# Head of a hybrid attention/pooling block: pooling weights fold first, mixer weights' two parts kept in DRAM for the second chunk

## The chip, the cores and the metric

One core of a Trainium2 chip runs one program. The metric is the device time of one execution in microseconds (us). Engines: PE (TensorE, matmul; PEld is its weight load), DVE (VectorE), ACT (ScalarE), POOL (GpSimd), SP (SyncE, which here issues every DMA). PSUM holds matmul results, SBUF everything else on the core, DRAM the rest.

## The reference, cut to what matters

```python
h = rmsnorm(x, attn_norm);  z = h @ w_in        # x: 2048 x 1024, fp32
u_pool, q, k, v, gates = split(z)               # 1024 | 16x64 | 2x64 | 2x64 | 2048
a = pool_mixer(u_pool)    # 4 groups of 256 channels: mean over the last 2/4/8/16 rows
                          # minus the row, then a 256x256 map per group (w_pool), scale
q, k = rope(rmsnorm(q)) / 8, rope(rmsnorm(k))   # rotary on 16 of 64 dims, by position
b = window attention(q, k, v)                   # window 128, 16 heads on 2 kv heads, sinks
x = x + (sigmoid(g_pool) * a + sigmoid(g_attn) * b) @ w_out
x = x + (silu(gate) * value) @ w_down           # up = causal conv3(rmsnorm(x) @ w_up)
```

## The kernel before

The 2048 rows are worked in two chunks of 1024. A chunk runs through a mixer (all of attention and pooling), the output projection, the up projection and the down projection. Activations lie transposed (channels on partitions), so a projection has a weight slab as its stationary operand and 512 columns of `h` as its moving one.

Every fp32 product is made of three passes. `split` writes a matrix as a high part (a cast on ACT to fp32r) and a low part (the difference, on DVE), and `mm3` multiplies high by high, high by low and low by high. A weight of 512 KB so becomes a tile of 1 MB in the pool "U" (19 buffers), which all big tiles share; raw weights arrive in the pool "R" (3 buffers). Other pools are "M" (5), "F" (4) and "Q" (4). Both chunks load and split the same mixer weights.

`Stream` serves the weights in the order of `weight_order()`: `get` of entry i issues the loads up to entry i+2 (`fetch`) and splits entries i+1 and i+2 (`part`), the latter often a little later. The pooling map is folded into the pooling part of `w_in` before its use: `fold(j)` multiplies half a group's input weights (`w_poolT[j]`) by the group's map (`w_pool`), 4 x 6 matmuls of 256 columns into two PSUM buffers "f", copies the sums to SBUF, and every second fold stores two slabs to `wfold` in DRAM, from which they are loaded later as slab kind "pu".

The mixer of a chunk first makes keys and values in 8 blocks of 128 rows (`raw`: 24 matmuls of 256 columns; `block`: norm, rotary, split; `turn`: transposes), with `first_fillers` between the blocks to keep PE busy: five of the eight folds and two slabs of the attention gate ("ga"). Then four groups of four heads follow, 8 items each, with gate slabs, pooling slabs and the other three folds between (`fillers`). A pooling slab of group g needs log2(window) doublings over 1024 columns on DVE, so one for group 0 and four for group 3; `windows` queues them in `slow`, two to a `run_later`.

In the program's head x arrives three times over: as `xT` in pieces for `h` (`make_h`, ACT for the high part and DVE for the low), and as rows for the sums of squares (`squares`, ACT), from which POOL makes the norm `r1` (`norm1`). `rope_tables` computes sine and cosine for all 16 blocks on DVE, with two Sin on ACT.

The order of instructions on each engine comes from a scheduling layer: program order is a priority, and it places an instruction where its tiles are expected to be free. Each engine then runs its own list strictly in order and waits on semaphores. That holds for SP too: a DMA that must wait for a buffer holds up those behind it.

Of the kernel before, what the change touches and what calls it, by code (L numbers as in the profile page):

```python
# [26 lines left out]
P = 128  # L27
# [17 lines left out]
FOLD_FIRST = 5  # L45


PRE = {0: 0, 1: 4}

# [23 lines left out]
class Stream:  # L73


    def __init__(self, entries, load, split):
        self.entries, self.load, self.split = entries, load, split
        self.raws, self.tiles = {}, {}
        self.used = self.loaded = self.parted = 0
# [29 lines left out]
def fillers(c, q4):  # L109

    ga = [[("ga", ct, n) for n in range(2)] for ct in (2 * q4 + 2, 2 * q4 + 3) if q4 < 3]
    pg = [[("pg", ct, n) for n in range(2)] for ct in (2 * q4 - 2, 2 * q4 - 1) if q4 > 0]
    pu = [[("pu", ct, n) for n in range(2)] for ct in (2 * q4, 2 * q4 + 1)]
    fold = [[("fold", j, 0)] for j in range(FOLD_FIRST, 8) if c == 0 and q4 == 0]
# [4 lines left out]
def first_fillers(c):  # L119

    ga = [("ga", ct, n) for ct in range(2) for n in range(2)]
    if c > 0:
        return [ga[0:1], [], ga[1:2], [], ga[2:3], [], ga[3:4], []]
    fold = [("fold", j, 0) for j in range(FOLD_FIRST)]
    return [fold[0:1], ga[0:1], fold[1:3], fold[3:4], fold[4:5], ga[1:2], ga[2:3], ga[3:4]]


def weight_order():
    out = []
    for c in range(NCH):  # L130
        if c > 0:
            out.append(("kv",))
        out += [(kind, j) for parts in first_fillers(c) for kind, j, n in parts if n == 0]
        out.append(("q", 0))
        for q4 in range(4):
            for n, parts in enumerate(fillers(c, q4)):
                if n == NB - 3 and q4 < 3:
                    out.append(("q", q4 + 1))
                out += [(kind, j) for kind, j, h in parts if h == 0]
        out += [("pg", ct) for ct in (6, 7)]  # L140
# [27 lines left out]
def block_kernel(ctx: ExitStack, tc: tile.TileContext, x, xT, pos, vec, qkn, w_poolT, w_pool, w_q, w_kv,  # L168
# [46 lines left out]

    def load_weights(kind, *a):
        if kind == "kv":
            srcs = [w_kv[:, 4 * j:4 * j + 4, :] for j in range(2)]
        elif kind == "q":
# [15 lines left out]
    def split_weights(key, raws):  # L235
# [4 lines left out]
        out = []  # L240
        for raw in raws:
            shape = [P, 2] + list(raw.shape)[1:]
            if key[0] in ("kv", "q"):
                out.append(up_.tile(shape, F32R, "U"))
            else:
                p, tag = (mp, "M") if out else (up_, "U")
# [79 lines left out]
    stream = Stream(weight_order(), load_weights, split_weights)  # L326
# [8 lines left out]
    posi = fp.tile([P, 16], I32, "F")  # L335
    load(posi, pos)
    vc = cp.tile([P, V_N], F32, "vc")
    load(vc, vec)

# [18 lines left out]

    def load_kv(i):
        raws.append(rp.tile([P, 4, 2 * P], F32, "R"))  # L360
# [9 lines left out]

    hs, kvw, raws = [], [], []
    for j in range(4):
        load_x0(j, 0, 256)
    for i in range(2):
        load_kv(i)
    gains = fp.tile([P, 2, HD], F32, "F")
    load(gains, qkn.rearrange("p (a d) -> p a d", a=2))
    make_h(0, 0, hs)
    for i in range(2):
        split_kv(i)  # L380
    stream.fetch(2)
# [4 lines left out]
    one = cp.tile([P, 1], F32, "one")  # L386
    V.memset(one, 1.0)
# [32 lines left out]
    tabs = {}  # L420

    def rope_tables():
        n = [P, 16, 8]
        posf = fp.tile([P, 16], F32, "F")
        V.tensor_copy(posf, posi)
        fr = fp.tile([P, 8], F32, "F")
        for i, f in enumerate(FREQ):
            V.memset(fr[:, i:i + 1], f)
        rt = up_.tile([P, 10, 16, 8], F32, "U")
# [7 lines left out]

        def reduced(dst, src, c):

            V.tensor_scalar(dst, src, c, None, op0=ALU.mult)  # L440
            rnd(s, dst)
            V.tensor_sub(dst, dst, s)
# [14 lines left out]
        for src, c in ((n0, a0), (n1, a1), (n2, a2), (n2, b2)):  # L457
            reduced(u, src, c)
            V.tensor_add(t, t, u)
        for i, off in ((8, 0.0), (9, 0.25)):  # L460
            V.tensor_scalar(u, t, off, None, op0=ALU.add)
            rnd(s, u)
            V.tensor_sub(u, u, s)
            V.tensor_scalar(u, u, 0.5 - 2.0**-25, -(0.5 - 2.0**-25), op0=ALU.min, op1=ALU.max)
            A.activation(rt[:, i], u, AF.Sin, scale=tau)
        sin, cos = rt[:, 8], rt[:, 9]

        gk = cp.tile([P, HD], F32, "gk")
        V.tensor_scalar(gk, gains[:, 1], 8.0, None, op0=ALU.mult)
        V.tensor_mul(gk[:, 16:HD], gk[:, 16:HD], gains[:, 0, 16:HD])  # L470
        tabs["gk"] = gk
        c = cp.tile([P, 16, 16], F32, "cq")
        sn = cp.tile([P, 16, 16], F32, "sq")
        for h in range(2):
            own = gains[:, 0, 8 * h:8 * h + 8].unsqueeze(1).to_broadcast(n)
            other = gains[:, 0, 8 - 8 * h:16 - 8 * h].unsqueeze(1).to_broadcast(n)
            V.tensor_tensor(c[:, :, 8 * h:8 * h + 8], cos, own, op=ALU.mult)
            V.tensor_tensor(sn[:, :, 8 * h:8 * h + 8], sin, other, op=ALU.mult)
        V.tensor_scalar(sn[:, :, 0:8], sn[:, :, 0:8], -1.0, None, op0=ALU.mult)
        tabs["q"] = (c, sn)  # L480
        ck = cp.tile([P, 16, 2, 8], F32, "ck")
# [921 lines left out]
```

## Time and profile before

| | |
|---|---|
| time, 3 runs | 2476.62, 2480.01 (median), 2482.35 us |
| profiled execution: its own time, its span | 2486.34 us, 2484.5 us |
| PE busy | 2433.9 us (98%) |
| DVE, ACT busy | 1967.4 us (79%), 1181.0 us (48%) |
| granted PE clock, mean | 0.996 |
| moved by DMA | 249.78 MB, mean 101 GB/s |

The span runs from the first to the last instruction; the profiled execution's own time is 1.8 us longer. Matmuls are pipelined: one of 512 columns reads as about 390 ns long, while they follow each other at about 227 ns, so group times are read as the busy time of the group and not as count times mean. The chunks' stages lie at: mixer 0 to about 540 us, output and up projection to about 1050, down projection to about 1270, then the same again.

### The profile page before, as it was taken

The page shows a single profiled execution, that of the slowest core. Times are in us where ns is not written, and L with a number is a line of the kernel's source. Part 1 is how long each engine was busy: PE and PEld are TensorE (multiplying, and loading weights), DVE is VectorE, ACT ScalarE, POOL GpSimd, SP SyncE. Part 2 cuts the span into 40 slices and gives each one's busy share as a digit, 9 for nine tenths or more (in the row PEclk, how much of TensorE's full clock was granted, in tenths as well). Part 3 has the DMA queues.
Part 4 walks back from the last instruction along what each step waited for, and adds up shares of the span by engine and source line. Part 5 has one row for each costly group of instructions (what it writes and reads, how often), then busy time and mean ns, then how long its engine had stood idle before and what let it go on. Part 6 is the DMA issues. An engine that isn't in the chain of part 4 may idle for free.

```text
span 2484.5 us, 32982 instructions
## 1 busy us (share of the span) xinstructions
PE 2433.9 (98%) x12224; PEld 2056.0 (83%) x12224; DVE 1967.4 (79%) x3528; ACT 1181.0 (48%) x2342; POOL 222.5 (9%) x217
## 2 busy tenths in 40 slices
PE   6999999999999999999999999999999999999999
PEld 6888888877888888788889888887788888887887
DVE  8776777885888788799966777778569788788994
ACT  6444444444455555543524444445435555454432
POOL 0122222200000000000002222222000000000000
PEclk9999999999999999999999999999999999999999
DMA  6221111038422233445231011110552222218321
GB/s 245 98 86 35 35 43 43 26 127 270 171 82 89 85 111 111 174 165 195 85 111 35 26 36 51 35 35 23 165 194 94 85 77 94 85 68 279 124 80 51
DMA packets 89871, 249.78 MB, mean 101 GB/s; under 512 B 9584, under 2 KB 11888, under 8 KB 87408
## 3 DMA queue, kind: packets, MB, share of 16 engines
q1 hardware_dynamic: 89712, 247.69, 28.9%
q8 instruction: 96, 1.57, 0.3%
q14 instruction: 63, 0.52, 0.1%
HBM read 196.28 MB, written 51.38 MB: 100 GB/s over the span
## 4 chain that ended last, share of the span: by engine, by line
PE 79%; DVE 13%; ACT 3%; DMA 2%; issue 2%; SPq 0%; POOL 0%; DVEq 0%; ACTq 0%; POOLq 0%
PE f L210 20%; PE f L954 18%; PE t L954 9%; PE a L210 6%; PE a L954 4%; PE f L1244 4%; PE a L1244 4%; PE t L1244 4%; PE s L1244 4%; ACT Q L711 1%; PE a L744 1%; PE s L690 1%; DVE F L794 1%; DVE U L195 1%; DVE U L840 1%
## 5 line engine op out<-in xcount | busy, mean ns | idle before, releaser
L210 PE MATMUL f<-U,U 128*128 128x512 f32 x3072 | 725.6, 393 | 8.9 <-ACT U L194 5.0
L210 PEld LDWEIGHTS f<-U,U 128*128 128x128 f32 x3072 | 573.6, 189 | 131.4 <-ACT U L194 8.6
L954 PE MATMUL f<-U,U 128*128 128x512 f32 x1512 | 359.7, 390 | 1.5 <-ACT Q L972 1.3
L954 PEld LDWEIGHTS f<-U,U 128*128 128x128 f32 x1512 | 283.4, 188 | 61.7 <-ACT Q L972 2.2
L1020 DVE SCALAR_TENSOR_TENSOR M<-F,vc,M 128x1024 f32<-128x1024 f32 x176 | 224.8, 1281 | 129.5 <-ACT M L1017 129.2
L210 PE MATMUL a<-U,U 128*128 128x256 f32 x1920 | 249.7, 285 | 12.9 <-ACT U L194 11.3
L210 PEld LDWEIGHTS a<-U,U 128*128 128x128 f32 x1920 | 242.4, 192 | 20.9 <-ACT U L194 11.3
L954 PE MATMUL t<-U,U 128*128 128x512 f32 x1080 | 254.2, 389 | 0.0
L954 PEld LDWEIGHTS t<-U,U 128*128 128x128 f32 x1080 | 202.7, 188 | 42.1
L711 ACT ACTIVATE Q<-s,st,r 128x128 f32<-128x128 f32 x256 | 114.4, 453 | 175.1 <-DVE st L706 167.4
L603 POOL TENSOR_TENSOR r<-r,mhalf 128x4 f32<-128x4 f32 (+1 forms) x80 | 77.2, 966 | 950.0 <-DVE r L602 888.3
L195 DVE TENSOR_TENSOR U<-R,U 128x512 fp32r<-128x512 f32 x214 | 146.3, 711 | 13.7 <-ACT U L194 12.8
L294 ACT CAST U<-R 128x1024 fp32r<-128x1024 f32 x120 | 125.4, 1053 | 65.9 <-DVE R L315 33.9
L295 DVE TENSOR_TENSOR U<-R,U 128x1024 fp32r<-128x1024 f32 x120 | 146.6, 1222 | 0.5 <-ACT U L294 0.5
L194 ACT CAST U<-R 128x512 fp32r<-128x512 f32 x214 | 123.2, 619 | 41.1 <-PE f L210 27.8
L954 PE MATMUL a<-U,U 128*128 128x512 f32 x576 | 138.6, 389 | 0.0
L954 PE MATMUL f<-U,M 128*128 128x512 f32 x504 | 123.9, 394 | 4.0 <-DVE F L998 4.0
L954 PEld LDWEIGHTS a<-U,U 128*128 128x128 f32 x576 | 108.0, 188 | 22.3
L1203 ACT CAST U<-U 128x1024 fp32r<-128x1024 f32 x74 | 77.2, 1051 | 86.2 <-PE a L1244 26.4
L954 PEld LDWEIGHTS f<-U,M 128*128 128x128 f32 x504 | 95.5, 190 | 24.8 <-DVE F L998 4.9
L1006 ACT COPY F<-f 128x512 f32<-128x512 f32 x42 | 24.7, 588 | 181.0 <-PE f L954 181.0
L1017 ACT ACTIVATE M<-F,vc 128x1024 f32<-128x1024 f32 x88 | 109.3, 1243 | 1.3
(253 smaller groups left out, 3902.5 us busy)
## 6 DMA issues: line engine op xcount, KB each, us to landing
R<-w_up SPq DMA_DIRECT2D x80, 512.0 KB, 3.3
actd<-M SPq DMA_DIRECT2D x44, 512.0 KB, 2.6
U<-w_down SPq DMA_DIRECT2D x88, 256.0 KB, 5.1
U<-actd SPq DMA_DIRECT2D x88, 256.0 KB, 5.4
R<-w_out SPq DMA_DIRECT2D x32, 512.0 KB, 4.3
U<-kept SPq DMA_DIRECT2D x12, 1024.0 KB, 7.8
R<-w_ga SPq DMA_DIRECT2D x16, 512.0 KB, 3.3
R<-w_q SPq DMA_DIRECT2D x16, 512.0 KB, 3.3
```

The lines of the kernel that those rows point to most:

```text
L194: A.copy(hi[:, t], src[:, t])
L195: V.tensor_sub(lo[:, t], src[:, t], hi[:, t].bitcast(F32))
L210: nc.tensor.matmul(out, a, b, start=(i == 0), stop=(i == n - 1))
L294: A.copy(t[:, 0], raw)
L295: V.tensor_sub(t[:, 1], raw, t[:, 0].bitcast(F32))
L603: G.tensor_tensor(r, r, mhalf[:, 0:nh], op=ALU.pow)
L711: A.activation(pr[:, h, :], sc[:, h, 0:P], AF.Exp, bias=nm[:, h:h + 1], scale=it["rq"][:, h:h + 1], accum_out=rs[:, h:h + 1])
L954: nc.tensor.matmul(bank, a[:, x, k, :], b[k // 2][:, y, k % 2, :], start=(first and i == 0), stop=(i == 11), skip_group_check=True)
L1017: A.activation(y, u[:, 2:], AF.Identity, bias=cw[:, 3, m:m + 1], scale=cw[:, 2, m:m + 1])
L1020: V.scalar_tensor_tensor(y, u[:, j:j + T], cw[:, j, m:m + 1], y, op0=ALU.mult, op1=ALU.add)
L1203: A.copy(hi, src)
L1244: nc.tensor.matmul(into[m], u[:, 0, c_], v[:, 1], start=(first and j == 0), stop=(k == n - 1 and j == 2), skip_group_check=True)
```

## The change

The head is laid out anew. `FOLDS` orders the folds by group from the last to the first, and the first four (groups 3 and 2) are done ahead of everything else; the other four all stand between the key and value blocks. Loads come in the order pooling weights, vectors, `xT`, more pooling weights, `w_kv`, rows of x. `fold` now fills one PSUM buffer with two of its four blocks and copies it with one DVE and one ACT instruction of 256 columns (before: two DVE copies of 128 columns for each block). `rope_tables` computes one chunk's 8 blocks, with fewer steps, and is called for the second chunk in the output projection of the first. A Sin on a constant is the first ACT instruction. The groups of heads and slabs run 3, 2, 1, 0. In chunk 0 each split mixer weight is also stored to DRAM (`keep_weights`), and chunk 1 loads the 1 MB of parts straight into a "U" tile; raw loads and splits of mixer weights disappear there.

```diff
-FOLD_FIRST = 5
+FOLD_LEAD = 4
+FOLD_FIRST = 8
+FOLDS = (6, 7, 4, 5, 2, 3, 0, 1)
@@ Stream.get
+        self.keep(key, self.tiles[i])
@@ first_fillers
-    fold = [("fold", j, 0) for j in range(FOLD_FIRST)]
-    return [fold[0:1], ga[0:1], fold[1:3], fold[3:4], fold[4:5], ga[1:2], ga[2:3], ga[3:4]]
+    fold = [("fold", j, 0) for j in FOLDS[FOLD_LEAD:FOLD_FIRST]]
+    return [[], fold[0:1], fold[1:2] + ga[0:1], fold[2:3] + ga[2:3] + fold[3:4], ga[1:2], [],
+            ga[3:4], []]
@@ load_weights, split_weights
+    def keep_weights(key, w):
+        if key[0] in ("fold", "none", "up", "out") or key in made:
+            return
+        made[key] = []
+        for i, t in enumerate(w if isinstance(w, list) else [w]):
+            name = "_".join(str(k) for k in key + (i,))
+            made[key].append(dp.tile(list(t.shape), F32, f"made_{name}"))
+            load(made[key][-1], t.bitcast(F32))
+        if (kind, *a) in made:
+            return None
+        if raws is None:
+            for src in made[key]:
+                out.append(up_.tile(list(src.shape), F32R, "U"))
+                load(out[-1].bitcast(F32), src)
+            return out if len(out) > 1 else out[0]
@@ head
-    posi = fp.tile([P, 16], I32, "F")
+    A.activation(cp.tile([P, 1], F32, "first"), one, AF.Sin)
+    raw = [rp.tile([P, 8, P], F32, "R") for _ in range(3)] + [mp.tile([P, 8, P], F32, "M")]
+    wg = fp.tile([P, 2, 2, 2 * P], F32, "F")
     load(posi, pos)
+    load(raw[0], w_poolT[lead[0]])
+    load(wg, w_pool[:, lead[2] // 2:lead[0] // 2 + 1])
     load(vc, vec)
+    load(raw[1], w_poolT[lead[1]])
...
     for j in range(4):
         load_x0(j, 0, 256)
+    for i in range(2, FOLD_LEAD):
+        load(raw[i], w_poolT[lead[i]])
     for i in range(2):
         load_kv(i)
-    make_h(0, 0, hs)
-    for i in range(2):
-        split_kv(i)
+    rows = [row(0, i) for i in range(4)]
@@ fold
-        for d in range(4):
-            pw = ps.tile([P, 512], F32, "f")[:, 0:256]
-            for m in range(2):
-                V.tensor_copy(o[m][:, 4 * half + d, :], pw[:, m * P:(m + 1) * P])
+        for d in range(0, 4, 2):
+            pw = ps.tile([P, 2, 2, P], F32, "f")
+            V.tensor_copy(o[0][:, 4 * half + d:4 * half + d + 2, :], pw[:, :, 0])
+            A.copy(o[1][:, 4 * half + d:4 * half + d + 2, :], pw[:, :, 1])
@@ out_proj
+                if c + 1 < NCH and n == 1 and m == 0:
+                    rope_tables(c + 1, load_gains())
@@ start of the program's work
-    rope_tables()
+    rope_tables(0, gains)
+    for i, j in enumerate(FOLDS[:FOLD_LEAD]):
+        fold(j)
+        if i == 1:
+            make_h(0, 0, hs)
+            for k in range(2):
+                split_kv(k)
```

Three places in the instruction lists. First PE at the start of the program; before, it begins with keys and values (`a_303`, `a_328` are the PSUM tiles of blocks 0 and 1, `U_127` and `U_132` the split `w_kv`, the other U tiles parts of `h`):

```order
L210 MATMUL a_303<-U_127,U_103 128x256
L210 MATMUL a_328<-U_127,U_103 128x256
L210 MATMUL a_303<-U_127,U_103 128x256 x2
L210 MATMUL a_303<-U_127,U_106 128x256 x3
L210 MATMUL a_303<-U_127,U_109 128x256 x3
```

Now it begins with folds (`f_...`, the two PSUM buffers in turn), and the first matmuls of keys and values (`a_456`, `a_481`) stand between the second fold and the third:

```order
L221 MATMUL f_251<-U_129,U_124 128x256 x11
L221 MATMUL f_266<-U_129,U_124 128x256 x11
L221 MATMUL f_286<-U_129,U_281 128x256 x12
L221 MATMUL f_301<-U_129,U_281 128x256 x12
L221 MATMUL a_456<-U_352,U_328 128x256
L221 MATMUL a_481<-U_352,U_328 128x256
L221 MATMUL f_366<-U_323,U_318 128x256 x12
L221 MATMUL f_381<-U_323,U_318 128x256 x12
```

So 48 matmuls of folds stand ahead of the first one that needs x. Second, ACT in the same stretch; before (the last two pieces of `h`, the split of `w_kv` from R_97 and R_99, the first fold's weights from R_135 and R_137, `h`, a square):

```order
L199 ACTIVATE U_121<-U_88,vc_91 128x256
L199 ACTIVATE U_124<-U_88,vc_91 128x256
L194 CAST U_127<-R_97 128x512 x2
L368 CAST U_132<-R_99 128x1024
L194 CAST U_141<-R_135 128x512 x2
L199 ACTIVATE U_103<-U_85,vc_91 128x256
L199 ACTIVATE U_106<-U_85,vc_91 128x256
L194 CAST M_146<-R_137 128x256 x2
L199 ACTIVATE U_109<-U_86,vc_91 128x256
L199 ACTIVATE U_112<-U_86,vc_91 128x256
L535 ACTIVATE M_283,ss_206<-M_283 128x1024
```

Now (R_93, R_94, R_95 are the raw weights of the first three folds, F_97 the two groups' maps, f_251 the first fold's first PSUM buffer):

```order
L366 ACT_TABLE_LOAD
L366 ACTIVATE first_91<-one_89 128x1
L205 CAST U_124<-R_93 128x512 x2
L205 CAST U_129<-F_97 128x256 x2
L205 CAST U_281<-R_94 128x512 x2
L205 CAST U_318<-R_95 128x512 x2
L205 CAST U_323<-F_97 128x256 x2
L210 ACTIVATE U_328<-U_85,vc_102 128x256
L210 ACTIVATE U_331<-U_85,vc_102 128x256
L210 ACTIVATE U_334<-U_86,vc_102 128x256
L607 COPY F_250<-f_251 128x256
```

The copy that frees the first PSUM buffer stands behind the cast of the third fold's weights R_95 and three pieces of `h`. Third, SP at the change of chunks; before (the last outputs of chunk 0, and raw loads for chunk 1):

```order
L188 DMA outT<-U_9958 128x512 x4
L188 DMA R_11215<-w_ga 128x1024
L188 DMA R_11298<-w_q 128x1024
L188 DMA R_11300<-w_q 128x1024
L188 DMA outT<-U_9817 128x512 x4
L188 DMA outT<-U_10179 128x512 x4
L188 DMA R_11575<-w_ga 128x1024
```

Now (`made_...` are the kept parts, loaded into U tiles):

```order
L199 DMA outT<-U_10020 128x512 x4
L199 DMA U_11261<-made_kv_6_1263 128x2048
L199 DMA U_11263<-made_kv_7_1265 128x2048
L199 DMA U_11265<-made_ga_0_4_738 128x2048
L199 DMA outT<-U_9879 128x512 x4
L199 DMA outT<-U_10241 128x512 x4
L199 DMA U_11371<-made_ga_0_5_911 128x2048
```

A load of parts needs a free U tile before it can be issued, where a raw load needed an R tile and the split afterwards needed the U tile.

## Rows read from the trace of the kernel before

**Rows 1.** The page, busy time of each engine: busy us, share, instructions.

```profile
PE 2433.9 (98%) x12224; PEld 2056.0 (83%) x12224; DVE 1967.4 (79%) x3528; ACT 1181.0 (48%) x2342; POOL 222.5 (9%) x217
```

**Rows 2.** Busy time by stage; after the stretch its length, then PE, PEld, DVE, ACT, POOL.

```profile
0.00:62.00 62.00, 42.29 (x272) 37.30 (x273) 50.11 (x235) 41.14 (x84) 5.01 (x11) 0.97 0.70 245
62.00:150.00 88.00, 84.13 (x557) 76.39 (x556) 68.17 (x236) 41.16 (x118) 17.77 (x18) 0.98 0.32 112
500.00:600.00 100.00, 94.83 (x408) 75.93 (x409) 72.59 (x107) 45.23 (x79) 7.09 (x5) 0.97 0.58 202
1250.00:1700.00 450.00, 448.17 (x2686) 395.43 (x2685) 328.13 (x887) 197.42 (x591) 99.85 (x97) 1.00 0.13 43
1700.00:1850.00 150.00, 144.92 (x678) 119.05 (x676) 98.40 (x152) 67.68 (x133) 11.25 (x9) 0.99 0.44 147
```

**Rows 3.** The same of the head; the last three: granted PE clock, DMA share, GB/s.

```profile
0.00:3.00 3.00, 0.00 (x0) 0.00 (x0) 1.00 (x32) 0.00 (x0) 0.72 (x6) 1.00 0.24 40
3.00:6.00 3.00, 0.00 (x0) 0.00 (x0) 0.36 (x3) 1.29 (x2) 0.00 (x0) 1.00 0.95 300
...
9.00:12.00 3.00, 0.69 (x2) 0.50 (x2) 1.83 (x6) 2.12 (x5) 0.00 (x0) 1.00 0.98 377
...
40.00:50.00 10.00, 9.90 (x79) 9.33 (x78) 9.74 (x43) 7.99 (x17) 0.81 (x2) 1.00 0.58 209
```

**Rows 4.** What PE waited for longest until 68 us: total us, times, longest.

```profile
PE a L210 <- ACT U L194: 11.3, 1, 11.3
```

**Rows 5.** Timeline: start, us, engine, line, operation, tiles, count, idle before and its releaser.

```profile
11.31 7.90 PE L210 MATMUL a<-U,U 128*128 128x256 f32 x48 [11.31 <-ACT U L194]
28.38 1.64 PE L516 MATMUL s<-identr,M 128*128 128x128 f32 x8 [4.78 <-DVE M L514]
...
592.40 0.69 DVE L879 SCALAR_TENSOR_TENSOR M<-f,F 128x512 f32<-128x512 f32 x1 [8.25 <-DMA R<-w_out]
```

**Rows 6.** The chain that ended last, head: start, us, what.

```profile
26.86 1.02 POOL r L498
31.63 1.28 ACT L465
32.93 0.32 ACT U L465
69.32 3.07 PE a L210 x24
109.16 4.04 DMA R<-w_poolT
```

**Rows 7.** Groups until 62 us: count, busy us, mean ns, idle before and releaser.

```profile
L194 ACT CAST U<-R 128x512 fp32r<-128x512 f32 x16 | 9.2, 615 | 4.0 <-DMA R<-w_ga 2.2 <-ACT U L194 0.8 <-DMA R<-w_poolT 0.4
L535 ACT ACTIVATE M<-M 128x1024 f32<-128x1024 f32 x8 | 8.4, 1057 | 5.3 <-DMA M<-x 5.0
L559 DVE COPY F<-f 128x128 f32<-128x128 f32 x32 | 8.2, 281 | 0.5 <-PE f L210 0.3
L195 DVE TENSOR_TENSOR U<-R,U 128x512 fp32r<-128x512 f32 x12 | 7.9, 687 | 0.6 <-ACT U L194 0.6
L199 ACT ACTIVATE U<-U,vc 128x256 fp32r<-128x256 f32 x16 | 7.0, 497 | 0.9 <-DMA U<-xT 0.8
```

**Rows 8.** What PE waited for from 480 to 545 us.

```profile
PE f L210 <- ACT U L194: 1.8, 1, 1.8
PE s L690 <- ACT Q L675: 1.3, 1, 1.3
PE a L744 <- POOL M L728: 0.9, 1, 0.9
```

**Rows 9.** A window doubling, groups from 150 to 530 us.

```profile
L794 DVE TENSOR_TENSOR F<-F 128x1036 f32<-128x1036 f32 x6 | 7.3, 1219 | 0.0
```

**Rows 10.** DMA issues of the page: KB each, median us from issue to landing.

```profile
U<-kept SPq DMA_DIRECT2D x12, 1024.0 KB, 7.8
```

**Rows 11.** The same from 1868 to 1876 us, where one such load runs alone.

```profile
U<-kept SPq DMA_DIRECT2D x1, 1024.0 KB, 4.8
```

More of the change, by code (lines that the diff above doesn't have):

```diff
@@ L106, in part, with slabs_of, fillers @@
             self.parted += 1
[L109 to L114, printed above, removed]
+def slabs_of(i):
+    return 6 - 2 * i, 7 - 2 * i
+def fillers(c, i):
+    ga = [[("ga", ct, n) for n in range(2)] for ct in slabs_of(i + 1) if i < 3]
+    pg = [[("pg", ct, n) for n in range(2)] for ct in slabs_of(i - 1) if i > 0]
+    pu = [[("pu", ct, n) for n in range(2)] for ct in slabs_of(i)]
+    fold = [[("fold", j, 0)] for j in FOLDS[FOLD_FIRST:] if c == 0 and i == 0]
     out = sum(ga[:1] + pg[:1] + fold + pu[:1] + ga[1:] + pg[1:] + pu[1:], [])
@@ L132, in weight_order @@
             out.append(("kv",))
+        else:
+            out += [("fold", j) for j in FOLDS[:FOLD_LEAD]]
         out += [(kind, j) for parts in first_fillers(c) for kind, j, n in parts if n == 0]
[L134 to L138, printed above, removed]
+        out.append(("q", 3))
+        for i in range(4):
+            for n, parts in enumerate(fillers(c, i)):
+                if n == NB - 3 and i < 3:
+                    out.append(("q", 2 - i))
                 out += [(kind, j) for kind, j, h in parts if h == 0]
-        out += [("pg", ct) for ct in (6, 7)]
+        out += [("pg", ct) for ct in slabs_of(3)]
         out += [("out", m) for n in range(2) for m in range(KT)]
@@ L214, in block_kernel @@
     slabs = {"ga": w_ga, "pu": wfold, "pg": w_gp, "out": w_out, "fold": w_poolT}
+    made = {}
+    def keep_weights(key, w):
[6 more added lines that the diff above has]
+            load(made[key][-1], t.bitcast(F32))
     def load_weights(kind, *a):
-        if kind == "kv":
-            srcs = [w_kv[:, 4 * j:4 * j + 4, :] for j in range(2)]
-        elif kind == "q":
+        if (kind, *a) in made:
+            return None
+        if kind == "q":
             srcs = [w_q[a[0], j] for j in range(2)]
@@ L369, in split_kv, with row @@
             V.tensor_sub(kvw[1][:, 1], raws[1], kvw[1][:, 0].bitcast(F32))
+    def row(c, n, p=mp, tag="M"):
+        t = p.tile([P, D], F32, tag)
+        load(t, x[(c * NB + n) * P:(c * NB + n + 1) * P, :])
+        return t
     hs, kvw, raws = [], [], []
@@ L529, in block_kernel, with squares @@
     ss = cp.tile([P, NCH, NB], F32, "ss")
-    def squares(c, n, p=mp, tag="M"):
-        t = p.tile([P, D], F32, tag)
-        load(t, x[(c * NB + n) * P:(c * NB + n + 1) * P, :])
+    def squares(c, n, t):
         A.activation(t, t, AF.Square, accum_out=ss[:, c, n:n + 1])
@@ L1263, in mixer @@
     def mixer(c, hs, kvw):
-        kts, vs, raw, block, turn = keys_values(c, hs, kvw)
-        ta, st = [], {}
+        kts, vs, raw, block_a, block_b, turn = keys_values(c, hs, kvw)
+        ta, st = {}, {}
         for n in range(NB):
             if c == 0 and n == 0:
-                for i in range(4):
-                    squares(0, i)
                 load_rest()
@@ L1275, in mixer @@
                 for i in range(4, NB):
-                    squares(0, i)
+                    squares(0, i, row(0, i))
             pk = [raw(0), raw(1)] if n == 0 else pk[1:] + ([raw(n + 1)] if n + 1 < NB else [])
+            fills = list(first_fillers(c)[n])
+            if c == 0 and n == 0:
+                for i in range(4):
+                    squares(0, i, rows[i])
             if c == 0 and n % 4 == 0:
@@ L1280, in mixer @@
                 spread(r1[:, 0, n:n + 4], n * P)
-            block(n, pk[0])
-            for f in first_fillers(c)[n]:
+            block_a(n, pk[0])
+            block_b(n)
+            for f in fills:
                 filler(*f, c, hs, ta, st)
-            if n > 0:
+            if n == 2 and c == 0:
+                turn(0)
+            if n > 1 or n == c == 1:
                 turn(n - 1)
@@ L1307, in mixer @@
             run_later()
-            parts = fillers(c, q4)[n]
+            parts = fillers(c, group)[n]
             for f in parts:
```

147 lines of the change are left out of this document (79 added, 68 removed).

## Prediction

> **What bounds the kernel now.** The page comes first: PE is busy 2433.9 of 2484.5 us [rows 1], and the change takes no matmul away. So nothing can be gained but the 50.6 us in which PE stands, and what its matmuls take too long. The table by stage says where that lies [rows 2]: 62.00 - 42.29 = 19.7 us before 62 us, 88.00 - 84.13 = 3.9 until 150, 5.2 from 500 to 600, 1.8 in the whole mixer of the second chunk (1250 to 1700), 5.1 from 1700 to 1850. The rest lies in stages that the change doesn't touch. DVE is near its limit only in places; in the head it is busy 9.74 of 10 us from 40 to 50 [rows 3]. PE's waits until 68 us begin with 11.3 us for the first split of `w_kv` [rows 4], and the timeline shows 4.78 at 28.38 for `M`, the norm `r1` spread for its matmuls [rows 5]. The chain shows `r1` done at 26.86 + 1.02 = 27.9 us [rows 6]. It waits for the rows of x: the squares on ACT (1.06 us each) stood 5.0 us idle for them [rows 7]. Before `r1` PE had had only 48 matmuls of keys and values and 24 of the first fold. At the chain's 3.07 us for 24 [rows 6], 0.128 each, these 72 are 9.2 us of work, so of the first 27.9 us 18.7 were lost. In them the first 48 took 7.90 us [rows 5], not 6.1.
>
> **The head.** What counts is when each list of instructions can go on.
>
> Start. The first fold needs positions, one raw weight and the maps: 8 + 512 + 512 KB, 1.06 MB. The trace moved 0.12 MB by 3 us and 0.30 MB a us after that [rows 3], so they are there at 3 + 0.94/0.30 = 6.1 us; a cast on ACT and a difference on DVE of half a map (half of 0.62 and 0.69 [rows 7], about 0.7 together) give 6.8 us against 11.3. The table load of ACT lies in the wait for data. So 4.5 us are won.
>
> First gap. The first fold's 24 matmuls at the pace of the first 48 (0.165 each) end at 10.8. The second fold needs the first one's PSUM buffer, and ACT's copy of it stands behind the cast of R_95. R_95 is the end of 3.34 MB of loads: 0.12 + 0.90 by 6 us, and what moved from 6 to 12 makes about 2.88 at 12 us; the remaining 0.46 at 0.38 MB a us [rows 3] comes at 13.2. Then ACT has two casts (1.2 less their overlap, 1.14), two of half the size (0.7), three pieces of `h` (0.46 each when they follow each other, from 7.0/16 busy [rows 7]) and the copy, which the trace doesn't show: bounded by the half cast and the DVE copy from below (0.28 for 128 columns) and by a cast of 512 from above (0.62), I take 0.4. So the second fold starts at 16.8, and PE stands 6.0 us. This gives back more than the start won.
>
> The norm. Up to the fourth square ACT still has five pieces of `h` (2.3), five copies (2.0), the casts of `w_kv` and of two more raw weights (four of some 1.1: 4.5) and four squares with their read-outs (1.25 each, 5.0): 16.8 + 13.8 = 30.6. With two small DVE steps, POOL's 1.02 and the spread of 0.43, `M` is there at 32.3, so `r1` comes 4 us later than now. But PE does more until then: four folds (96) and both blocks (48), 144 matmuls at 0.123 (their pace in long runs, a little under the chain's 0.128) = 17.7 us, which it can finish at about 32.6. Lost by then: 14.9. Before, at the same kind of point: 18.7 until `r1`, 19.6 at the spread (28.38 [rows 5] less 8.8, the 72 at the same 0.123). Won: 4.7 us.
>
> After the norm. The next keys need a PSUM buffer "a" that is free only after block 0's norm (1.8 us of waiting by the same sort of count), and then DVE's list, in which rotary steps, low parts of `h` and block 1 stand mixed, holds PE for about 4, plus about 3 for matmuls that start slowly after a stop and for the later blocks. That is 9 against the 10 that the trace loses from 28.4 to 92 us. DVE's own load falls: a fold's copies go from eight of 0.28 to two of about 0.45 plus two on ACT, so from 2.2 to 0.9 us, five times in this stretch; rotary steps have 64 elements for 128 and there are fewer before the first block needs them. I take 1.2 won.
>
> Folds later. The three folds that stood between attention items are gone from there. That stretch has 3.9 us of PE standing and a wait for `w_poolT` of 4.04 us in the chain [rows 2, 6]; 2 of it go, since other stops stay. Together 4.7 + 1.2 + 2 = 8 us. Bounds: -2 (slower), if DVE's list after the norm costs 10 more than counted; 16, if the first gap closes and nothing takes its place.
>
> **The ends of the mixers.** The last group is now the one with window 2. In the trace the last group is that of window 16, so six doublings of 1.22 us [rows 9] (four against one, for two slabs) leave DVE's list where PE waits 1.8 + 1.3 + 0.9 = 4.0 us for it and for what stands behind it [rows 8]. I take somewhat under half, 1.75, and the same for the second chunk, whose stage stands 5.1 us [rows 2]: 3.5; bounds 0 and 9. The doublings now fall in the first group, where the folds have left.
>
> **Parts from DRAM.** In the second chunk 34 splits go, each two casts of 0.62 and two differences of 0.69 [rows 7]: 42 us of ACT and 47 of DVE. But PE stands 1.8 us in those 450 [rows 2], so at most 1.8 is to be had: 0.5. What can be late is a load: it is issued only when a U tile is free. By the order of the built program nearly every load has 19 us or more of PE work between that and its first matmul. Two (pg slabs 7 and 5) have 4 transposes, 4 matmuls of p times v, 24 of queries, 4 transposes and 4 of scores, about 5.1 us. One such load alone took 4.8 us to land [rows 11], with others beside it 7.8 [rows 10]. So from nothing to 2 x 2.7 = 5.4 us; the two neighbours in the order are issued 2.5 us later, so it is nearly alone, and I take 0. The kept parts' writes, 34 MB in the first chunk, run while the tiles are still in use, in a stage like that of the second chunk, where DMA is 0.13 busy [rows 2].
>
> A rule of the Trainium skill ("DMA: Bandwidth & Descriptors", section Bandwidth) gives 6.15 us for a transfer of 1 MB, as the time its engines are busy. By the 4.8 us of [rows 11], landing included, the sum is as above; by the page it would be two waits of about 1 us more, so 2 us less gain.
>
> **Rotary tables.** For the second chunk some 45 small DVE steps and two Sin stand in the first chunk's output projection; a copy of 128 columns takes 0.28 [rows 7], so the steps take 12 us at most, and about 6 at half the size, the value I take. They stand where DVE stood 8.25 us for data [rows 5]; they are hidden there, and cost up to 4 us if that wait is gone: 0.5. A Sin changes ACT's table and the next Tanh changes it back: four loads in place of three, of 1.28 us each [rows 6], all in ACT's slack but the one at 31.63 that goes.
>
> The Trainium skill ("ScalarE: Activation LUTs", What ACT_TABLE_LOAD costs) counts 1.38 us of draining on top of the 1.28. In the trace the Sin starts at 32.93, 0.02 behind its load's end [rows 6], so no such time shows; by the page the added load would cost 2.7 us of ACT, still beside PE's work, and the sum would stay.
>
> **Sum.** 8 + 3.5 + 0.5 - 0.5 = 11.5 us off the profiled execution's 2486.3 (span and 1.8 around it): 2474.8. The median of the runs is 6.3 below that execution, so I forecast 2480 - 11.5 = 2468.5, rounded to 2469.
>
> **Rivals.** (1) *Won at the start, given back before the keys.* The lists on ACT and DVE bind the head, not the order of loads: `r1` comes at 32 or later, and all eight blocks follow it. For it: DVE's 9.74 of 10 us, the copy behind R_95. Against it: PE has 17.7 us of work ahead of `r1` in place of 9. Then only the ends and some of the later folds' stops remain, 3 us: 2477.
>
> (2) *Slower: ACT becomes the bound of the head.* ACT gets 16 copies of fold sums (6.4 us) and the casts of three more folds (3 x 1.2 and maps) into the stretch before the first queries, and PE's two fold buffers are freed only through ACT's list. It decides from the point where each fold waits for ACT more than a fold's own 3 us. If `r1` slips to 40 us (R_95 at 17 us, copies at 0.6, two squares late), PE has stood 40 - 17.7 = 22 us by then, 3 more than now, and the four folds' copies after that hold DVE and ACT for 4 more; with the ends at 2, 5 us slower: 2485. Against it: ACT was busy 41 of 62 us [rows 2].
>
> (3) *The loads of parts come late.* Both short ones at 7.8 us and a table wait of 2: 7 of the 11.5 go, 2476. For it: one queue in strict order, each load of double size. Against: DMA 0.13 busy there.
>
> **How the numbers follow.** Forecast 0.65, its own range 2461 to 2475; rival 1 0.18, rival 2 0.07, rival 3 0.10. About 0.2% (5 us) is what a measurement of this kernel tells from no change, so faster is below 2475. Of the forecast 0.60 lies there, of rival 3 0.05 and of rival 1 0.05: 0.70. Slower, above 2485, are half of rival 2 and a little of rival 1: 0.06. The rest, 0.24, is the same. The range of 8 in 10 is the forecast's own with rivals 1 and 3 and the head's upper bound taken in: 2459 to 2480.
>
> **What would show it.** Right: PE's first matmul near 6.8 us, a stop of some 6 us from 10.8 to 16.8 whose releaser is ACT's copy; the norm on POOL near 31; the second chunk's mixer with as few stops of PE as before and less DVE; fewer waits from 480 to 545. Wrong: the second fold starts near 12 (then the head gains 16), or PE stands more than 23 us by the time it reaches the first queries, or waits on made tiles above 1 us.

## The result, and the profile after

The changed kernel takes 2463.9 us (2463.6 to 2466.2), the kernel before 2480.1; the ratio is 0.9936, with an interval of 0.9924 to 0.9947. Run once more beside other kernels (e8 below) it took 2463.7, ratio 0.9931 (0.9919 to 0.9942). The forecast was 2469, 11.5 us less; measured are 16 to 17 less. The direction and the range hold, the size is short by nearly a third, and the terms of the sum are wrong in an instructive way. One of e7's six executions took 4041.2 us at a mean granted clock of 0.557 and is left out of its time.

The page's first part and two stages, columns as in [rows 1, 2]:

```profile
PE 2426.2 (98%) x12224; PEld 2056.7 (83%) x12224; DVE 1928.2 (78%) x3452; ACT 1151.1 (47%) x2294; POOL 225.1 (9%) x217
```

```profile
0.00:62.00 62.00, 48.41 (x336) 45.87 (x337) 49.05 (x208) 42.40 (x97) 5.55 (x11) 0.97 0.89 327
62.00:150.00 88.00, 87.77 (x558) 78.58 (x557) 66.83 (x215) 44.31 (x130) 17.40 (x18) 1.00 0.51 198
```

In the first 62 us PE now runs 336 matmuls where it ran 272, and from 62 to 150 it stands 0.2 us in place of 3.9. Stretches of clock time can't be compared in the second chunk, which begins some 15 us earlier now. The mixer of chunk 1, taken from its first keys to its last queries, is the same work in every kernel; before (e12), changed (e8), and two variants from below, the changed kernel without kept parts (e1) and with the old order of groups (e2):

```profile
1265.93:1699.90 433.97, 432.16 (x2629) 383.12 (x2628) 323.86 (x883) 198.84 (x601) 99.72 (x97) 1.00 0.12 39
1251.39:1684.50 433.11, 430.84 (x2629) 383.16 (x2627) 297.41 (x830) 169.15 (x541) 101.18 (x97) 1.00 0.21 78
1251.10:1686.80 435.70, 431.99 (x2628) 382.83 (x2627) 330.10 (x890) 198.59 (x601) 102.37 (x97) 1.00 0.12 39
1254.60:1685.50 430.90, 430.71 (x2629) 383.13 (x2627) 289.26 (x822) 168.83 (x540) 99.05 (x97) 1.00 0.21 78
```

PE's busy time of the same matmuls is 432.2 and 432.0 us where weights are split there, 430.8 and 430.7 where their parts are loaded: the busy time of pipelined matmuls holds waits inside it.

Where the time went is best read from when PE reaches the same instruction. The places are the last query matmul of the first chunk ("queries end"), the first up-projection matmul into bank "a", the first keys of chunk 1, the same two of chunk 1, and the end of the span. Both kernels have two profiles:

| PE reaches, us | queries end | up | chunk 1 | queries end | up | end |
|---|---|---|---|---|---|---|
| before, first profile | 488.8 | 639.2 | 1270.0 | 1703.9 | 1850.0 | 2484.5 |
| before, second (e12) | 488.0 | 635.7 | 1265.9 | 1699.9 | 1844.0 | 2476.6 |
| changed, first | 474.0 | 621.5 | 1253.6 | 1686.9 | 1829.3 | 2464.0 |
| changed, second (e8) | 473.3 | 620.8 | 1251.4 | 1684.5 | 1826.9 | 2459.9 |

The first pair differs by 20.5 us, more than the medians do; the second by 16.7, as the medians do. By the second pair 14.7 us are won until the first queries are done, nothing more until chunk 1 begins (14.5), and 2.6 in the mixer and output projection of chunk 1 (17.1). So nine tenths are won before the first chunk's last queries: 0.4 us and 72 more matmuls, 8.9 us at 0.123 each, by the first scores (98.6 for 99.0), and the rest, 5.5, from there (374.7 us for 389.1, which held those 72).

The chain's head, and PE's waits until 68 us, answering [rows 6] and [rows 4]:

```profile
6.53 6.12 DMA R<-w_poolT
...
15.62 0.26 ACT F L607
15.93 3.17 PE f L221 x24
...
28.45 1.27 POOL r L547
```

```profile
PE f L221 <- ACT U L205: 7.0, 1, 7.0
PE f L221 <- DVE U L206: 3.1, 2, 2.8
PE f L221 <- ACT F L607: 2.2, 2, 1.7
PE a L221 <- DVE M L500: 1.3, 1, 1.3
```

The norm's power on POOL comes at 28.45, 1.6 us later than before (26.86 in [rows 6]), and PE has done far more by then. The timeline of PE, and of DVE in the same stretch (start, us, engine, line, operation, tiles, count, idle before and its releaser):

```profile
6.99 0.80 PE L221 MATMUL f<-U,U 128*128 128x256 f32 x2 [6.99 <-ACT U L205]
10.55 4.86 PE L221 MATMUL f<-U,U 128*128 128x256 f32 x22 [2.76 <-DVE U L206]
15.93 3.17 PE L221 MATMUL f<-U,U 128*128 128x256 f32 x24 [0.52 <-ACT F L607]
...
30.66 1.06 PE L565 MATMUL s<-identr,M 128*128 128x128 f32 x8
```

```profile
8.52 0.20 DVE L463 TENSOR_SCALAR gk<-Q 128x64 f32<-128x64 f32 x1 [1.18 <-DMA Q<-qkn]
8.75 0.21 DVE L464 TENSOR_TENSOR gk<-gk,Q 128x48 f32<-128x48 f32 x1
8.87 1.28 DVE L206 TENSOR_TENSOR U<-R,U 128x512 fp32r<-128x512 f32 x2
...
27.97 0.16 DVE L544 TENSOR_SCALAR r<-ss 128x4 f32<-128x4 f32 x1
```

PE starts at 6.99, stops 2.76 us inside the first fold for a low part on DVE (which stood behind the scaling of a gain whose load came late), and from 15.93 to 30.66 it does not stop. The spread norm, at 28.38 in [rows 5], is now at 30.66. `L544` is the norm's first step on DVE; the experiments turn on it.

### The profile page after: what moved, and what is told of

The parts are those of the page before. It is cut to its first block, busy times and chain, and to the rows that moved or that the text cites. A ratio compares the mean times of both kernels' runs of the same rounds, so it can differ in the third digit from the quotient of the medians.

```text
span 2464.0 us, 32845 instructions
## 1 busy us (share of the span) xinstructions
PE 2426.2 (98%) x12224; PEld 2056.7 (83%) x12224; DVE 1928.2 (78%) x3452; ACT 1151.1 (47%) x2294; POOL 225.1 (9%) x217
## 4 chain that ended last, share of the span: by engine, by line
PE 83%; DVE 10%; ACT 3%; issue 1%; DMA 1%; POOL 0%; SPq 0%; DVEq 0%; ACTq 0%
PE f L221 22%; PE f L1009 18%; PE t L1009 9%; PE a L221 6%; PE a L1009 4%; PE a L1299 4%; PE f L1299 4%; PE s L1299 4%; PE t L1299 4%; ACT Q L763 2%; PE s L742 1%; PE a L796 1%; DVE F L846 1%; PE t L774 1%; DVE U L206 1%
## 5 line engine op out<-in xcount | busy, mean ns | idle before, releaser
L221 PE MATMUL f<-U,U 128*128 128x512 f32 (+1 forms) x3168 | 735.8, 390 | 15.6 <-ACT U L205 8.3
L221 PEld LDWEIGHTS f<-U,U 128*128 128x128 f32 x3168 | 585.7, 190 | 136.9 <-DVE U L206 10.5
L1009 PE MATMUL f<-U,U 128*128 128x512 f32 x1512 | 359.8, 390 | 1.3 <-ACT Q L1027 1.3
L1009 PEld LDWEIGHTS f<-U,U 128*128 128x128 f32 x1512 | 283.5, 188 | 61.5 <-ACT Q L1027 2.2
L323 DVE TENSOR_TENSOR U<-R,U 128x1024 fp32r<-128x1024 f32 x120 | 146.7, 1222 | 0.0
L206 DVE TENSOR_TENSOR U<-R,U 128x512 fp32r<-128x512 f32 x142 | 93.9, 691 | 7.8 <-ACT U L205 7.2
L1259 DVE TENSOR_TENSOR U<-U,U 128x1024 fp32r<-128x1024 f32 x74 | 89.7, 1220 | 10.3 <-ACT U L1258 10.3
```

Of the source, the lines that this page charges most:

```text
L206: V.tensor_sub(lo[:, t], src[:, t], hi[:, t].bitcast(F32))
L221: nc.tensor.matmul(out, a, b, start=(i == 0), stop=(i == n - 1))
L323: V.tensor_sub(t[:, 1], raw, t[:, 0].bitcast(F32))
L1009: nc.tensor.matmul(bank, a[:, x, k, :], b[k // 2][:, y, k % 2, :], start=(first and i == 0), stop=(i == 11), skip_group_check=True)
L1259: V.tensor_sub(lo, src, hi.bitcast(F32))
```

## The experiments

Three ideas were to be told apart: the prediction's (an earlier start and work ahead of the norm, ends of the mixers), a second in which DVE's list in the head is what counts, and a third in which the kept parts relieve the second chunk. The diffs are shortened, and `...` marks what is left out.

**e1: no kept parts.**

```diff
 def keep_weights(key, w):
-    if key[0] in ("fold", "none", "up", "out") or key in made:
-        return
+    return
...
 def load_weights(kind, *a):
+    if kind == "kv": srcs = [w_kv[:, 4 * j:4 * j + 4, :] for j in range(2)]
...
```

> The changed kernel with raw loads and splits of the mixer weights in the second chunk again; nothing is kept in DRAM. Theory: PE waited for almost nothing in that chunk's mixer, so the 34 splits were hidden: 2464 us, as the changed kernel, within 2. Rival: DVE and ACT, relieved of 47 and 42 us, are what shortened the second chunk (4 us less than before from its first matmul to its last): 2468.

Measured: 2466.9 (2465.1 to 2468.3), ratio 0.9946 (0.9932 to 0.9960), so 3 us above the changed kernel's 2463.7, at the edge of what the intervals tell apart. The trace says where: from chunk 1's first keys to its up projection 579.4 us pass (1251.1 to 1830.5), in the changed kernel 575.7 and 575.5. The other profiles bear it out: the stretch takes 575.5 to 576.0 in all nine with kept parts, and 578.1 to 580.0 in the five without (before, e12, e1, e3, e11). The theory that the splits were hidden falls; the rival's 4 is near.

**e2 and e3: the order of groups.** e2 is the changed kernel with groups 0 to 3, e3 the kernel before with 3 to 0.

```diff
-FOLDS = (6, 7, 4, 5, 2, 3, 0, 1)      # e2; e3 adds these lines to before
+FOLDS = (0, 1, 2, 3, 4, 5, 6, 7)
...
 def slabs_of(i):
-    return 6 - 2 * i, 7 - 2 * i
+    return 2 * i, 2 * i + 1
...
```

> The changed kernel with groups, slabs and folds in their old order (window 2 first, window 16 last). Theory: the end of each mixer waits for the doublings of the last group; the two traces differ by 3.8 and 2.1 us from the last product of p and v to the first matmul of the up projection, so 6 us come back: 2470. Rival: the ends were shortened by other things (folds gone, less work on DVE): 2464 to 2465.

Measured: 2465.7 (2463.3 to 2468.6), ratio 0.9941 (0.9928 to 0.9953). What it gives back stands in the head: the queries of chunk 0 end at 476.7, 3 us later than in the changed kernel. From there to the up projection it needs 147.0 us, the changed kernel 147.5, and for chunk 1's stretch 575.9 against 575.5. The rival is nearer. But that stretch hides two effects. With the reversed order chunk 1's end, from the last queries to the up projection, is 2.6 us shorter (142.4 for 145.0), and its mixer is 2.2 us longer (433.1 for 430.9): PE stops there twice, 1.17 and 1.1 us, for steps of the softmax that stand in DVE's list behind the last steps of a slab of window 16, now in the first group, where e2 has no stop. The first stop (timelines of DVE and PE, e8):

```profile
1355.17 1.64 DVE L846 TENSOR_TENSOR F<-F 128x1024 f32<-128x1024 f32 x1
...
1361.52 0.63 PE L774 MATMUL t<-identr,Q 128*128 128x128 f32 x4 [1.17 <-DVE Q L767]
```

> The kernel before with the order of groups, slabs and folds reversed and nothing else. Theory: 6 us less than before, 2474; at least 3.5, the size predicted. Rival: no change, 2480, since the six doublings of each chunk fall into the first group, where before's three late folds still stand between the items and want DVE too.

Measured: 2478.5 (2474.3 to 2480.1), ratio 0.9990 (0.9981 to 0.9999): 1.4 us. Reversal alone is worth between nothing and 5 us. Its chunk 1 shows the same exchange: the end is 0.5 us shorter than in e12 (143.6 for 144.1) and the mixer 1.8 longer (435.8 for 434.0). The ends were also over-read: of the 3.8 us that the first pair of profiles differed from the last product of p and v to the up projection, 2.7 were in the first profile of before only; in its second (e12) that way takes 116.2 us, in the changed kernel 115.1.

**e4: three folds between attention items again.**

```diff
-FOLD_FIRST = 8
+FOLD_FIRST = 5
```

> The changed kernel with only one of the last four folds between the key blocks and three among the attention items, as before had three there. Theory: what PE lost between 92 and 150 us before (5.7 us against 0.8 now, from the pace of its matmuls) was these three folds: 5 us come back, 2469. Rival, by the prediction's own price: 2 us, 2466. Second rival: the keys need the folds as cover, and it is 7 or more.

Measured: 2462.8 (2461.0 to 2465.7), ratio 0.9931 (0.9918 to 0.9943): as the changed kernel, so all three ideas fall. Late folds cost nothing in the changed kernel. From 68 to 150 us its PE waits but 0.5 us:

```profile
PE a L796 <- POOL M L780: 0.5, 1, 0.5
```

**e5: keys first, then the four folds**, with loads in that order.

```diff
+    for i in range(2): load_kv(i)            # ahead of the folds' weights
     load(raw[0], w_poolT[lead[0]])
...
+    pk = [raw(0), raw(1)]; for j in FOLDS[:FOLD_LEAD]: fold(j)
...
-    for j in FOLDS[:FOLD_LEAD]: fold(j)      # ahead of everything
...
```

> The changed kernel with keys and values of blocks 0 and 1 ahead of the four folds, and the loads in that order (xT and w_kv, then the folds' weights, then rows of x); all else as changed. Theory: what counts is PE's work ahead of the norm, 144 matmuls in place of 72, in whichever order; PE starts at about 11.3 us as before, and loses 14 to 15 us until the spread norm in place of 13.2: 1.5 us slower than the changed kernel, 2465.5. Rival: the earlier start is the gain, and 4.3 us come back: 2468.5.

Measured: 2473.8 (2471.7 to 2474.9), ratio 0.9971 (0.9960 to 0.9981): 10 us back, more than either idea. PE starts at 11.06 as expected, and the norm's first step on DVE comes at 29.56. But the copy that spreads the norm had got a place in DVE's list behind 16 pieces of `h` and four differences of weights, and PE ran dry. DVE's copy, and PE's stops (timelines):

```profile
43.75 0.43 DVE L560 COPY M<-r 128x512 f32<-128x512 f32 x1
```

```profile
40.11 0.80 PE L221 MATMUL f<-M,U 128*128 128x256 f32 x2 [7.62 <-ACT M L205]
43.56 1.01 PE L221 MATMUL f<-M,U 128*128 128x256 f32 x3 [2.66 <-DVE M L206]
44.37 1.94 PE L562 MATMUL s<-identr,M 128*128 128x128 f32 x8
```

So it does not price the earlier start by itself; it shows what a late place of one DVE instruction costs.

**e6, e9, e10: the relief of DVE undone**, both parts (e6), copies alone (e9), tables alone (e10, the second chunk's in a U tile).

```diff
-            V.tensor_copy(o[0][...d:d + 2, :], pw[:, :, 0])
-            A.copy(o[1][...d:d + 2, :], pw[:, :, 1])
+            for e in range(2):                     # e6, e9
+                for m in range(2):
+                    V.tensor_copy(o[m][:, 4 * half + d + e, :], pw[:, e, m])
...
     rope_tables(0, gains)
+    rope_tables(1, gains)                          # e6, e10
```

> The changed kernel with fold sums copied by DVE alone, eight copies of 128 columns a fold as before, and the rotary tables of both chunks made in the head. It adds some 11 us of copies and 6 us of table steps to DVE in the first 100 us. Theory: DVE's list is what holds PE after the norm (before lost 26.5 us from the spread norm to the last queries, the changed kernel 18.2), so 4 to 8 us come back: 2468 to 2472. Rival: the 8.3 us are due to the order of the work and DVE has room: 2464 to 2466.

> The changed kernel with the fold sums copied by DVE alone, eight copies of 128 columns a fold as before; the tables as changed. Theory: DVE's list in the head binds, so the 12.5 us that both edits cost together divide by the DVE time that each adds ahead of the norm: four folds' copies (some 5 us) and the second chunk's tables (some 7 us), so 5 us here: 2469. Rival: copies are the whole, since they also hold the two PSUM buffers: 10 or more, 2474. Second rival: nothing, 2464.

> The changed kernel with the rotary tables of both chunks made in the head, the second chunk's in a U tile, the copies as changed. Theory: 7 us, 2471, and the norm's first step on DVE some 7 to 9 us later than in the changed kernel. Rival: the small steps fit between DVE's waits and cost nothing: 2464 to 2465.

Measured: e6 2476.2 (2472.3 to 2479.5), ratio 0.9981 (0.9972 to 0.9989); e9 2472.0 (2467.7 to 2473.1), ratio 0.9962 (0.9950 to 0.9975); e10 2469.9 (2468.6 to 2471.2), ratio 0.9958 (0.9946 to 0.9971). So 12.5, 8 and 6 us come back, in e6 more than the theory's 4 to 8. The five runs of e9 lie 5 us apart, so 8 and 6 are not told apart; the traces of both have 6. All of it is lost ahead of the first scores, which PE reaches at 98.6 in the changed kernel (e8), 104.9 in e9, 105.0 in e10 and 112.0 in e6; from there to the last queries all four take 374.7 us. The last square's read-out on ACT ends at 27.5 in the changed kernel and at 25.9, 27.6 and 26.4 in e9, e10 and e6: the sums of squares are there in time. The norm's first step on DVE (timelines of e9, e10, e6):

```profile
36.02 0.16 DVE L544 TENSOR_SCALAR r<-ss 128x4 f32<-128x4 f32 x1
```

```profile
36.15 0.17 DVE L545 TENSOR_SCALAR r<-ss 128x4 f32<-128x4 f32 x1
```

```profile
43.41 0.17 DVE L544 TENSOR_SCALAR r<-ss 128x4 f32<-128x4 f32 x1
```

It waits for its turn: from 26 to 36 us DVE is busy 10.00 of 10 us in e6 and e9 and 9.73 in e10. PE does have gaps; the row of e6 (columns as in [rows 2], the third from the end the granted clock):

```profile
26.00:36.00 10.00, 7.55 (x48) 6.96 (x48) 10.00 (x67) 7.10 (x18) 0.00 (x0) 0.84 1.04 364
```

The step is DVE's 88th instruction in the changed kernel, behind 18.9 us of busy time; in e9 the 146th behind 27.1, in e10 the 165th behind 27.7, in e6 the 198th behind 32.8. Its start moves by 8.0, 8.2 and 15.4 us, the end of the queries by 6, 6 and 13. Only part of that is added work (for e9 32 copies of 0.28 for 8 of 0.42, 5.6 us): the rest are some 30 steps of the first chunk's own rotary tables and two differences of a split, which stood behind the step and which the scheduling layer now sets ahead of it.

**e7: loads of w_kv ahead of the third fold's**, gains later.

```diff
-    gains = load_gains()
...
     for j in range(4): load_x0(j, 0, 256)
+    gains = load_gains()
+    for i in range(2): load_kv(i)
     for i in range(2, FOLD_LEAD): load(raw[i], w_poolT[lead[i]])
-    for i in range(2): load_kv(i)
```

> The changed kernel with w_kv loaded ahead of the third and fourth fold's weights, and the q and k gains behind xT. In the instruction lists both copies of the first fold's sums now stand ahead of the cast and difference of the third fold's weights, and the scaling of the gains behind the first fold's low parts. Theory: in the changed kernel the first fold stood 2.8 us for DVE's low part, which stood behind the scaling, and the second was freed by ACT's copy; both go, the head loses 2 to 3 us less until the norm: 2461.5. Rival: the third fold's weights come 1 MB later, their split holds PE in turn, and nothing is won: 2464.

Measured: 2465.3 (2461.9 to 2466.6), ratio 0.9934 (0.9921 to 0.9947): the rival's result, by another way. The gap ahead of the second fold is closed (first row), but the norm's step on DVE comes at 29.91, 1.9 us later, and its spread 3.6 us later.

```profile
10.02 9.02 PE L221 MATMUL f<-U,U 128*128 128x256 f32 x50 [2.38 <-DVE U L206]
...
34.27 1.06 PE L564 MATMUL s<-identr,M 128*128 128x128 f32 x8
```

**e8, e12: both kernels again**, as they are.

> The changed kernel once more, as it is, so that the other runs have it beside them on the same chip: 2464 us; its profile shows how far one stage's losses differ between executions.

> The kernel before once more, for a second profile: its first one was 6 us above the median. Expected: 2480, the losses until the last queries as in the first profile (19.6 and 26.5 us), and 8 to 10 us between the last product of p and v and the up projection in place of 12.8, as the other variants show there.

Measured: 2463.7 (2462.1 to 2465.4), and 2478.6 for the one execution of before; their traces are the table's second rows. The first profile of before had lost 0.8 us more until the queries' end, 2.7 more from there to the up projection and 4.4 after it: scatter, which the first comparison credited to the change.

**e11: the kernel before with the relief alone.**

```diff
-        for d in range(4): ... # eight copies of 128 columns on DVE
+        for d in range(0, 4, 2): ... V.tensor_copy(..., pw[:, :, 0]); A.copy(..., pw[:, :, 1])
-    rope_tables()
+    rope_tables(0, gains)      # chunk 1's in out_proj, as in the change
...
-        rt = up_.tile([P, 10, 16, 8], F32, "U")
+        rt = mp.tile([P, 12, NB, 8], F32, "M")
...
```

> The kernel before with two parts of the change alone: fold copies shared by DVE and ACT in two of 256 columns, and each chunk's own rotary tables. Order of loads, folds and groups as before. Theory: DVE's list binds the head of the kernel before too, so half or more of the change's 16 us come by this alone: 2470 to 2472. Rival: the relief pays only where four folds stand ahead of the norm: 2477 to 2480.

Measured: 2478.4 (2475.8 to 2480.7), ratio 0.9994 (0.9985 to 1.0003): the rival. The trace shows both sides of it. The relief works: from 100 to 150 us PE waits 0.6 us in one place, where before (e12) it waited 2.7 in two. These are the waits of e11 and of e12 from 68 to 150 us:

```profile
PE a L742 <- POOL M L726: 0.6, 1, 0.6
```

```profile
PE a L744 <- POOL M L728: 2.7, 2, 2.0
```

But the norm's spreading copy comes 4 to 5 us later than before (32.2 for 27.9 and 27.2), and PE, which has 72 matmuls ahead of it and no more, stands 9.6 us for it. Two things delay it. The loads of four rows of x are issued over 9.41 us in e11, over 2.40 in e12: the fourth waits until 23.88, just after the first square's read-out. By the two kernels' text that is the want of an "M" buffer, since the tables' work tile, in "U" before, now takes one of the five that the rows and the fold's map need; that this is the reason was not tested. The last square so ends at 28.6 for 25.3. Then the norm's second step on DVE stands behind a rotary step that waits for a Sin. These are SP in e11 and in e12, ACT and DVE in e11, and PE's wait until 68 us:

```profile
14.79 9.41 SPq L188 DMA_DIRECT2D M<-x  x4
14.64 2.40 SPq L188 DMA_DIRECT2D M<-x  x4
27.48 1.06 ACT L532 ACTIVATE M<-M 128x1024 f32<-128x1024 f32 x1 [1.01 <-DMA M<-x]
30.23 0.23 DVE L473 SCALAR_TENSOR_TENSOR M<-M 128x64 f32<-128x64 f32 x1 [1.40 <-ACT ck L475]
```

```profile
PE s L513 <- DVE M L511: 11.2, 2, 9.6
```

So e11 loses 5.0 us more than e12 until the spread norm (32.67 for 27.63, 72 matmuls done in both) and wins 6.4 from there to the last queries (454.0 for 460.4): its "no change" is a gain and a loss.

Together these runs fill a square (e6 has groups and parts as changed; e2 moves the queries' end by 3 us, e1 by less than 1). The queries of chunk 0 end at

| | relief of DVE undone | with relief |
|---|---|---|
| one fold ahead of the norm | 488.0 (before) | 486.7 (e11) |
| four folds, leading | 486.7 (e6) | 473.3 (changed) |

Either half alone measures as 1.3 us, both as 14.7. Leading folds lengthen DVE's list ahead of the norm, and the relief takes that length back; this half e6, e9 and e10 show. The other half is open: the relief alone wins 6.4 us after the norm, and whether it would keep them without e11's late row of x, which the changed kernel doesn't have, was not run.

## Why the prediction was right, and where it was wrong

*Start.* Predicted 6.8, measured 6.99; the 4.3 us are there.

*First gap.* Predicted: the second fold at 16.8, behind ACT's copy and the cast of R_95. Measured: 15.93, released by that copy, which stands where the list has it. R_95's cast began at 12.66, not 13.2: in the first 12 us 3.4 MB came. But the stop of 6 us from 10.8 is not there. PE stopped earlier, for DVE's low part (2.76): the step's sum left out what else stands in DVE's list ahead of that part. It then ran the rest of the first fold slowly (22 matmuls in 4.86 us). The time lost by then, 15.93 less 24 matmuls at the prediction's 0.123, is 13.0; the step had 13.8.

*The norm.* Predicted 32.3 for `M`, measured 30.66; the loss until the spread norm (start less the 144 matmuls begun by then, at 0.123 each) 12.9 for 14.9. The second profile has 31.44 and 13.7. The mechanism holds: in e11, without that work, PE stands 9.6 us for the norm.

*After the norm, and folds later.* These two steps failed in size and the second in its reason. Predicted 1.2 + 2 us. Measured: of the 14.7 us at the queries' end 5 to 7 are won until the norm and 8 to 10 after it. The step "DVE's own load falls" priced the copies and smaller rotary steps at 1.2 by their own time. e9 and e10 give 8 and 6 us for undoing one of them, e6 12.5 for both, because a DVE list that is full delays whatever stands last in it by all that is put ahead; and that is paid ahead of the first scores, on the way to the norm above all, where the step had put none of it. And the folds' place among the attention items, to which the other 2 were put down, is worth nothing (e4): what PE stood for from 100 to 140 us in [rows 6] went in e11 as well, with the late folds left where they were.

*The ends of the mixers.* Predicted 3.5, measured about nothing: 147.0 against 147.5 us in e2, 1.4 us in all in e3. In chunk 1 the end did become 2.6 us shorter (e2), but the step gave the doublings' new place no price, and they cost 2.2 there. In chunk 0 the waits remain, with the same releasers. From 465 to 530 us in the changed kernel, answering [rows 8]:

```profile
PE s L742 <- ACT Q L727: 1.8, 1, 1.8
PE a L796 <- POOL M L783: 1.2, 1, 1.2
PE f L221 <- DVE U L206: 0.7, 1, 0.7
```

The largest end on ACT and POOL, for the last item's queries and masks, not on doublings; so they did in [rows 8], which the step read as waits for DVE's list.

*Parts from DRAM.* Predicted 0.5, with 1.8 us as the most there was, since PE stood no longer. Measured 3 us by the time (e1) and 3.8 by the stretch. The cap was wrong: standing time is no bound, since the same matmuls of that mixer read 432.0 us busy without kept parts (e1) and 430.8 with them (e8). Nor was 1.8 the standing to be won, since the reversed order had raised it to 3.7 (e1), of which the parts took 1.4 away. No load of a part is among PE's waits in that mixer; rival 3 fell. The loads landed as [rows 11] said (page's columns, from 1250 to 1700 us):

```profile
U<-made_q SPq DMA_DIRECT2D x8, 1024.0 KB, 4.7
U<-made_pu SPq DMA_DIRECT2D x8, 1024.0 KB, 4.8
U<-made_pg SPq DMA_DIRECT2D x8, 1024.0 KB, 4.8
U<-made_ga SPq DMA_DIRECT2D x7, 1024.0 KB, 6.6
```

*Rotary tables.* Predicted a cost of 0.5 where they go. There they cost at most some 1 us: DVE works on them from 565 to 574 us, and queries to up projection takes 147.5 us in the changed kernel, 147.7 before (e12), and 146.5 and 146.7 in e6 and e10, which don't have them there. Where they leave they are worth 6 (e10). The step looked only at the place they came to.

*Rivals.* Rival 1 named the right engine lists and the wrong outcome. Rival 2 had the right kind of mechanism, a list through which the folds are freed, on the wrong engine: ACT's list grew and DVE's decided, as e6 shows at 2476.

*The sum.* Head 8 against 14.7, ends 3.5 against about 0, parts 0.5 against 2.6 to 3.8, tables -0.5 against 0 to -1 at their new place. Two errors of opposite sign brought the total nearer than its terms, which is luck.

What stays open: why the scheduling layer sets pieces of `h` (e5) or table steps (e9) ahead of the norm's steps when DVE's list grows, and what the relief alone is worth. A version with the norm's two DVE steps forced early was not tried, nor were the head's smaller edits by themselves (the key block in two steps, the Sin on a constant, raw `w_kv` in a "U" tile); e6, which has them all, takes 2476. No variant beats the changed kernel beyond the intervals; e4 is level with it.

## What to carry to other kernels

Where engines run strict lists, price a moved step by the last instruction in the list that others wait for, not by its own duration: small table steps that keep DVE for some 9 us cost 6 us of PE in a full list, and at most 1 where that list has room. Two edits that each measure as nothing came to 15 us together, so undo them one by one and both at once, and find where each "nothing" comes from: e11's was a gain of 6 and a loss of 5. Compare the same work, not the same stretch of clock time. And take a second profile before dividing a gain among stages: here 4 of 20 us were scatter of the first.

## What the runs showed of the hardware

- Copying from PSUM by DVE took 0.28 us for 128 columns [rows 7] and 0.42 for 256, by ACT 0.37 for 256, so two blocks take DVE 0.42 in one copy and 0.56 in two (groups until 62 us, changed kernel):

```profile
L606 DVE COPY F<-f 128x256 f32<-128x256 f32 x13 | 5.5, 422 | 3.0 <-PE f L221 2.8
L607 ACT COPY F<-f 128x256 f32<-128x256 f32 x13 | 4.7, 368 | 2.3 <-DVE F L606 2.3
```

- The head's loads ran at 420 GB/s from 12 to 20 us, where 377 is the most in [rows 3]; and 34 MB of writes beside the first mixer (DMA share 0.30 from 150 to 500 us in place of 0.11) cost it some 1 us at most (queries end at 472.8 in e1 without them, at 474.0 and 473.3 with them). The row of the changed kernel, last column GB/s:

```profile
12.00:20.00 8.00, 7.48 (x50) 7.27 (x50) 6.32 (x17) 7.33 (x18) 0.00 (x0) 1.00 1.03 420
```

- In e5 PE stands from 32.5 to 40.1 us, and the granted clock reads 0.50 from 38 to 46 us, which is 1.2 GHz, the lower of its two levels (the other is 2.4), and 1.00 from 48 us. A stop so costs more than its length: nine matmuls of 256 columns took 1.78 us from 45.97, 0.2 each where 0.12 is the pace. In the head of the changed kernel it reads 1.00 throughout in the second profile; in the first it reads 0.83, a mean of the two levels, from 40 to 50 us. The stretches in e5, third from the end the granted clock:

```profile
38.00:40.00 2.00, 0.00 (x0) 0.00 (x0) 2.00 (x6) 2.00 (x6) 0.00 (x0) 0.50 0.17 68
44.00:46.00 2.00, 2.00 (x12) 2.00 (x11) 2.00 (x9) 0.52 (x2) 0.09 (x1) 0.50 0.87 297
48.00:50.00 2.00, 2.00 (x19) 2.00 (x18) 1.93 (x11) 1.51 (x5) 0.00 (x0) 1.00 1.01 374
```
